# Reading the moving operand of the split products from the last column to the first, in a hybrid decoder layer on one core

## The chip, the cores and the metric

The kernel runs on one core of one Trainium2 chip. Its metric is the device time of one launch in microseconds; three timed runs of the kernel before have a median of 2824.08 us (2821.2 to 2825.72). The core's engines work side by side, each through a queue of its own: TensorE (PE, with its weight loads as PEld) does matrix products, VectorE (DVE) and ScalarE (ACT) work element by element, GpSimd (POOL) and SyncE (SP) mostly issue transfers. TensorE reads its operands from SBUF and writes its sums to banks of PSUM, 128 partitions by 512 fp32 columns each.

## The reference

One step of a decoder layer for a prompt of 2048 tokens and for eight samples of four tokens each, with a model width of 1024, in fp32. What matters here are the dense products:

```python
q, k, v, g, glr, z, xbc, dt_raw = jnp.split(hn @ lw['w_in'], cuts, axis=-1)
...
mixed = jnp.concatenate([o_gla, y], axis=-1).astype(hn.dtype) @ lw['w_out']
...
q = (hn @ w_xq).reshape(b, t, XA_HEADS, XA_HEAD_DIM).astype(jnp.float32)
s = jnp.einsum('bthd,bmhd->bhtm', q, mk.astype(jnp.float32)) * (XA_HEAD_DIM ** -0.5)
p = jax.nn.softmax(s, axis=-1)
o = jnp.einsum('bhtm,bmhd->bthd', p, mv.astype(jnp.float32)).reshape(b, t, D_MODEL)
return o.astype(hn.dtype) @ w_xo
...
f = (jax.nn.silu(hf @ lw['w_gate']) * (hf @ lw['w_up'])) @ lw['w_down']
```

Between them stand a gated linear attention and a state space scan in chunks, norms and activations. The results are the layer's output for both groups and the states that are carried on.

## The kernel before, in words

**Split products.** An fp32 operand x is kept as two parts of the type fp32r, a larger one (ScalarE's copy, `xh`, `whi`, `r` or `s`) and a smaller one (VectorE's difference between x and the larger, `xl`, `wlo`, `e` or again `s`, `r`). A product is then the sum of three matmuls, larger by larger, larger by smaller, smaller by larger. The helper `three` (L132) issues them: L134, L135 and L136, each with the stationary operand (`wh` or `wl`, 128 x 128) loaded first and the moving operand (`ah` or `al`) streamed past it, 256 to 512 columns, into the same columns of one PSUM bank. Only the first of a sum overwrites the bank; the others add to it.

**First part of the program (to about 854 us).** The prompt goes through in blocks of 512 tokens. For each, `fm` and `tm` (L542, L683) make the input projection into four banks `acc`: `fm` streams the tokens past the weights, `tm` the weights past the tokens. In between stand the pieces of the memory tokens' keys and values (`memory`, L349, banks `mx`, 256 columns), folds of the attention weights (`folds`, L438 and `last_folds`, L471), and the scans in plain fp32.

**Second part.** The output projection, the attention's scores and values, and the three products of the feed-forward part are done in passes over one kind of work each. A unit of it is a product of 2 x 2 blocks made of seven block products in place of eight, with sums and differences of blocks as operands; the results of the seven gather in the banks `accA` (two buffers), `accB` and `accC`. The moving operands, weights in `r` and `e`, have 512, 384 or 272 columns. One loop over `order` issues the matmuls of a block product through `three`, then calls the steps that empty the banks (`evs`), split the next operands (`part`) and bring in side work such as the transposes at L1858 and the samples. The order of issue on each engine follows this program text, pinned by `pin`.

**Waits.** The framework derives the waits from which tiles an instruction reads and writes. A matmul can wait on a semaphore itself; one with more waits than it can hold has an EVENT_SEMAPHORE instruction ahead of it in TensorE's queue. TensorE also waits for itself in places, on its own semaphore.

Of the kernel before, what the change touches and what calls it, by code (L numbers as in the profile page):

```python
# [42 lines left out]
def hymba_kernel(ctx: ExitStack, tc: tile.TileContext, a: dict, o: dict, dbg: dict | None = None):  # L43
# [87 lines left out]

    def three(ps, wh, wl, ah, al, start, stop, more=False):  # L132

        nc.tensor.matmul(ps, lhsT=wh, rhs=ah, start=start, stop=False, skip_group_check=more)  # L134
        nc.tensor.matmul(ps, lhsT=wh, rhs=al, start=False, stop=False, skip_group_check=more)  # L135
        nc.tensor.matmul(ps, lhsT=wl, rhs=ah, start=False, stop=stop, skip_group_check=more)  # L136
# [212 lines left out]
    def memory():  # L349
      with ExitStack() as mctx:  # L350
# [47 lines left out]
        for which, weights in enumerate((a["w_xk"], a["w_xv"])):  # L398
            for u in range(8):
                _, wh, wl = wload(weights[u], 2, pm if u % 2 else None, raws=pm)  # L400
                ps = mxt()
                for kt in range(KT):
                    k0 = kt * P
                    three(ps[:, 0:MEM], wh[:, k0:k0 + P], wl[:, k0:k0 + P], mh[:, kt], ml[:, kt], kt == 0, kt == KT - 1)
                raw = mt_([P, MEM], "kraw", bufs=2)
                nc.vector.tensor_tensor(raw, ps[:, 0:MEM], rbm, op=ALU.mult)
                nc.gpsimd.dma_start(out=kv[which, u], in_=raw)
                yield
# [29 lines left out]
    def folds():  # L438
# [3 lines left out]
        def fold_qk(n, h, Kh, Kl):  # L442
            pss = [acct() for _ in range(2)]
            _, wh, wl = wload(a["w_xqT"][n, h])
            for kt in range(4):
                c = (kt % 2) * MEM
                for d in range(2):
                    k0 = d * 512 + kt * P
                    three(pss[kt // 2][:, c:c + MEM], wh[:, k0:k0 + P], wl[:, k0:k0 + P], Kh[:, d], Kl[:, d], d == 0, d == 1)
            for u in range(2):  # L450
                t = pa2.tile([P, 512], F32, name="fold", bufs=2)
                for k in range(2):
                    kt = 4 * n + 2 * u + k
                    nc.scalar.activation(t[:, k * MEM:(k + 1) * MEM], pss[u][:, k * MEM:(k + 1) * MEM], AF.Copy, scale=gq[:, kt:kt + 1])
                c = (h % 2) * MEM
                nc.gpsimd.dma_start(out=wqk[h // 2, 2 * n + u][:, :, c:c + MEM], in_=t.rearrange("p (k m) -> p k m", m=MEM))
# [14 lines left out]
    def last_folds():  # L471
# [32 lines left out]
        for i in range(8):  # L504
            h, n = divmod(i, 2)
            if i + 1 < 8:
                split(i + 1)
            wh, wl = ws[n]
            pss = [mxt() if i == 7 else acct() for _ in range(2)]
            for mt in range(2):  # L510
                for d in range(2):
                    ms = slice(mt * P, (mt + 1) * P)
                    three(pss[mt], xc[:, 0, h, d, ms], xc[:, 1, h, d, ms], wh[d], wl[d], d == 0, d == 1)
            for mt in range(2):
                names = "fold", "fold", "fraw", "fh", "fl"
                t = pa2.tile([P, 512], F32R, name=names[(2 * i + mt) % 5], bufs=2 if (2 * i + mt) % 5 < 2 else None)
                nc.scalar.copy(f(t), pss[mt])
                nc.gpsimd.dma_start(out=wvo[n, h][:, mt], in_=f(t))
            yield
# [1746 lines left out]
    for e, (n, i) in enumerate(order):  # L2266
# [46 lines left out]
        ps = banks[n, {1: "B", 3: "C", 5: "C"}.get(i, "A")]  # L2313
# [134 lines left out]
```

## Time and profile before

| | |
|---|---|
| timed runs, median | 2824.08 us (2821.2 to 2825.72, 3 runs) |
| profiled execution, span from the first to the last instruction | 2826.9 us |
| mean granted TensorE clock | 0.991 |
| TensorE busy / its weight loads | 2737.6 us / 2366.6 us |
| VectorE / ScalarE / GpSimd busy | 2080.6 us / 1472.1 us / 536.4 us |
| TensorE instructions (matmuls) | 15,207 |
| DMA | 512.17 MB, 181 GB/s on average |

The profiled execution has no time of its own beside its span, which is 0.1% over the timed median. A row of the groups by line reads: line, engine, operation, tile written <- tiles read, shape (contraction*rows, then partitions x columns of the result) and count, then busy microseconds, mean nanoseconds of one, and idle time ahead of them. Matmuls are pipelined: the duration of one runs from its start to a modelled end and overlaps the next, so what one adds to the time is the distance from its start to the next start. A row of the timeline begins with its start and its duration in microseconds. A row of the view by stretches reads: stretch, its length, busy time and count of PE, then of PEld, then granted clock, DMA share and GB/s.

### The profile page before, as it was taken

How to read it: one execution, taken by the hardware profiler on the slowest of the kernel's cores; microseconds unless marked ns; L12 is line 12 of the kernel's file. 1: busy time of each engine (PE TensorE's matmuls, PEld its weight loads, DVE VectorE, ACT ScalarE, POOL GpSimd, SP SyncE). 2: the span in 40 equal slices, each digit the busy share in tenths (PEclk: the TensorE clock that was granted, in tenths of full speed). 3: DMA queues.
4: the chain of work that ended last, by engine and by line, in shares of the span. 5: the costliest groups of instructions: out<-in, count | busy, mean ns of one | idle time of the engine just before them, and what ended most of it. 6: DMA issues, size and time to landing. Idle time of an engine off the chain costs nothing.

```text
span 2826.9 us, 41830 instructions
## 1 busy us (share of the span) xinstructions
PE 2737.6 (97%) x15207; PEld 2366.6 (84%) x15207; DVE 2080.6 (74%) x3831; ACT 1472.1 (52%) x2921; POOL 536.4 (19%) x722
## 2 busy tenths in 40 slices
PE   8999999999998999999899999999999999999998
PEld 8987887787876878878799888899999997788786
DVE  7677677776757787677888787767677878574776
ACT  5545554554546687777755434434445555353432
POOL 2142332321322321015321210001000001000011
PEclk9999999999999999999999999999999999999999
DMA  7345535343266886468765567775244436464765
GB/s 254 116 139 187 150 104 159 117 132 89 82 206 232 283 284 225 147 189 252 266 211 184 176 243 239 256 253 176 97 138 174 151 120 209 176 211 99 236 156 128
DMA packets 151102, 512.17 MB, mean 181 GB/s; under 512 B 18176, under 2 KB 29488, under 8 KB 137328
## 3 DMA queue, kind: packets, MB, share of 16 engines
q1 hardware_dynamic: 94560, 331.81, 35.7%
q0 software_dynamic: 44240, 152.82, 17.0%
q10 hardware_dynamic: 12096, 24.86, 2.7%
q8 instruction: 120, 1.97, 0.3%
q14 instruction: 86, 0.70, 0.1%
HBM read 365.76 MB, written 143.67 MB: 180 GB/s over the span
## 4 chain that ended last, share of the span: by engine, by line
PE 76%; DVE 11%; ACT 5%; issue 3%; DMA 3%; POOL 1%; DVEq 0%; SPq 0%; POOLq 0%; ACTq 0%
PE accA L134 9%; PE accA L135 9%; PE accA L136 9%; PE accC L134 5%; PE acc L134 5%; PE acc L136 5%; PE acc L135 5%; PE accC L136 5%; PE accC L135 5%; PE accB L134 2%; PE accB L136 2%; PE accB L135 2%; DVE s L1665 2%; DVE sum L1645 1%; ACT r L1734 1%
## 5 line engine op out<-in xcount | busy, mean ns | idle before, releaser
L134 PE MATMUL accA<-r,s 128*128 128x512 f32 (+2 forms) x1792 | 637.6, 356 | 20.0 <-ACT r L1734 8.6
L136 PE MATMUL accA<-r,s 128*128 128x512 f32 (+2 forms) x1792 | 629.1, 351 | 2.8 <-DVE s L1665 2.7
L135 PE MATMUL accA<-r,s 128*128 128x384 f32 (+2 forms) x1472 | 502.8, 342 | 1.7 <-DVE r L1738 1.7
L134 PEld LDWEIGHTS accA<-r,s 128*128 128x128 f32 x1792 | 338.7, 189 | 72.6 <-ACT r L1734 12.2
L1663 ACT ACTIVATE s<-sum 128x512 fp32r<-128x512 f32 (+1 forms) x456 | 282.6, 620 | 220.1 <-DVE sum L1645 107.5
L136 PEld LDWEIGHTS accA<-r,s 128*128 128x128 f32 x1792 | 339.1, 189 | 34.0 <-DVE s L1665 4.0
L134 PE MATMUL accC<-r,s 128*128 128x512 f32 (+2 forms) x896 | 319.7, 357 | 8.8 <-ACT sg L1972 3.1
L1665 DVE TENSOR_TENSOR s<-sum,s 128x512 fp32r<-128x512 f32 (+1 forms) x456 | 305.7, 677 | 20.2 <-ACT s L1663 19.9
L136 PE MATMUL accC<-r,s 128*128 128x512 f32 (+2 forms) x896 | 314.8, 351 | 0.0
L135 PEld LDWEIGHTS accA<-r,s 128*128 128x128 f32 x1472 | 278.8, 189 | 19.0 <-DVE r L1738 2.9
L1665 DVE TENSOR_TENSOR s<-raw,s 128x512 fp32r<-128x512 f32 (+1 forms) x342 | 234.0, 684 | 51.5 <-ACT s L1663 50.4
L135 PE MATMUL accC<-r,s 128*128 128x384 f32 (+2 forms) x736 | 251.9, 342 | 0.5 <-DVE r L1738 0.5
L1663 ACT ACTIVATE s<-raw 128x512 fp32r<-128x512 f32 (+1 forms) x342 | 213.3, 624 | 72.7 <-PE accC L136 50.7
L128 ACT ACTIVATE whi<-wraw 128x1024 fp32r<-128x1024 f32 (+2 forms) x140 | 128.8, 934 | 187.3 <-PE acc L135 111.8
L134 PEld LDWEIGHTS accC<-r,s 128*128 128x128 f32 x896 | 170.1, 190 | 37.2 <-ACT s L1663 6.9
L129 DVE TENSOR_TENSOR wlo<-wraw,whi 128x1024 fp32r<-128x1024 f32 (+2 forms) x140 | 153.5, 1108 | 50.9 <-ACT whi L128 50.2
L136 PEld LDWEIGHTS accC<-r,s 128*128 128x128 f32 x896 | 170.0, 190 | 15.5 <-DVE s L1665 0.4
L142 POOL TENSOR_TENSOR rs<-ms,nhalf 128x1 f32<-128x1 f32 (+4 forms) x125 | 111.9, 896 | 361.2 <-DVE ms L140 344.9
L134 PE MATMUL acc<-xh,whi 128*128 128x512 f32 (+1 forms) x464 | 168.9, 365 | 8.7 <-ACT xh L289 8.4
L136 PE MATMUL acc<-xh,wlo 128*128 128x512 f32 (+1 forms) x464 | 164.9, 357 | 1.7 <-DVE wlo L129 1.7
L135 PE MATMUL acc<-xl,whi 128*128 128x512 f32 (+1 forms) x464 | 164.5, 356 | 0.2 <-DVE xl L290 0.2
L1645 DVE TENSOR_TENSOR sum<-raw 128x512 f32<-128x512 f32 (+1 forms) x228 | 156.5, 686 | 3.6
(698 smaller groups left out, 5876.5 us busy)
## 6 DMA issues: line engine op xcount, KB each, us to landing
raw<-in_w_gu_dram SPq DMA_DIRECT2D x66, 1024.0 KB, 4.9
wraw<-in_w_in_fm_dram SPq DMA_DIRECT2D x52, 512.0 KB, 3.7
wraw<-in_w_in_tm_dram SPq DMA_DIRECT2D x48, 512.0 KB, 3.9
st<-in_w_down_dram SPq DMA_DIRECT2D x37, 512.0 KB, 6.0
aT<-og POOLq DMA_DIRECT2D x22, 768.0 KB, 4.8
raw<-aT SPq DMA_DIRECT2D x16, 1024.0 KB, 6.2
out_y_dram<-y POOLq DMA_DIRECT2D x28, 512.0 KB, 6.2
yp<-y POOLq DMA_DIRECT2D x28, 512.0 KB, 6.3
```

What stands on the lines that cost most here:

```text
L128: last[0] = nc.scalar.activation(hi[:, cs], raw[:, cs], AF.Copy)
L129: nc.vector.tensor_tensor(lo[:, cs], raw[:, cs], f(hi)[:, cs], op=ALU.subtract)
L134: nc.tensor.matmul(ps, lhsT=wh, rhs=ah, start=start, stop=False, skip_group_check=more)
L135: nc.tensor.matmul(ps, lhsT=wh, rhs=al, start=False, stop=False, skip_group_check=more)
L136: nc.tensor.matmul(ps, lhsT=wl, rhs=ah, start=False, stop=stop, skip_group_check=more)
L142: nc.gpsimd.tensor_tensor(out=rs[:rows, :cols], in0=ms[:rows, :cols], in1=nhalf[:rows, :cols], op=ALU.pow)
L1645: nc.vector.tensor_tensor(t[out], x, y, op=o)
L1663: nc.scalar.activation(h3, v, AF.Copy)
L1665: return lambda: nc.vector.tensor_tensor(l3, v, f(h3), op=ALU.subtract)
L1734: nc.scalar.activation(hi, v, AF.Copy)
```

## The change

In `three`, ahead of the three matmuls, the accumulator and the two moving operands are replaced by views of themselves whose columns run backwards: the access starts at the last column and goes on with step -1. The stationary operands stay. Since the moving operand and the result are reversed alike, each column's sum lands where it did before.

```diff
@@ -131,6 +131,7 @@
 
     def three(ps, wh, wl, ah, al, start, stop, more=False):
 
+        ps, ah, al = (t[:, ::-1] for t in (ps, ah, al))
         nc.tensor.matmul(ps, lhsT=wh, rhs=ah, start=start, stop=False, skip_group_check=more)
         nc.tensor.matmul(ps, lhsT=wh, rhs=al, start=False, stop=False, skip_group_check=more)
         nc.tensor.matmul(ps, lhsT=wl, rhs=ah, start=False, stop=stop, skip_group_check=more)
```

Every call of `three` is reached, 12,672 matmuls. Other matmuls are left as they are. The added line moves L134 to L136 to L135 to L137 in the changed file.

The order of instructions on each engine is the same before and after. What differs is where TensorE waits for its own earlier work. One such place is the passes of the second part, where a block product ends in `accA` and the next begins in `accB`. Before:

```order
L134 MATMUL accA<-r_8425,s 128x512
L135 MATMUL accA<-e_8426,s 128x512
L136 MATMUL accA<-r_8425,s 128x512
L134 MATMUL accB<-r_8151,s 128x512
L135 MATMUL accB<-r_8151,s 128x512
L136 MATMUL accB<-r_8151,s 128x512
```

With the change:

```order
L135 MATMUL accA<-r_8425,s 128x512
L136 MATMUL accA<-e_8426,s 128x512
L137 MATMUL accA<-r_8425,s 128x512
L135 MATMUL accB<-r_8151,s 128x512 [waits PE_49]
L136 MATMUL accB<-r_8151,s 128x512
L137 MATMUL accB<-r_8151,s 128x512
```

The matmuls stand as they did; the first one into `accB` now waits on TensorE's own semaphore. Over the program 114 matmuls gain such a wait and 71 groups lose theirs, most of the latter at the transposes of L1858; the waits of the other engines are the same.

## The prediction

> **What bounds the kernel now.** I read the page from the top: the busy shares, then the chain that ended last, then the groups by line and shape, then stretches of the timeline in which matmuls follow each other without a break. The first two say which engine sets the time.
>
> ```profile
> span 2826.9 us, 41830 instructions
> PE 2737.6 (97%) x15207; PEld 2366.6 (84%) x15207; DVE 2080.6 (74%) x3831; ACT 1472.1 (52%) x2921; POOL 536.4 (19%) x722
> PE 76%; DVE 11%; ACT 5%; issue 3%; DMA 3%; POOL 1%; DVEq 0%; SPq 0%; POOLq 0%; ACTq 0%
> PE accA L134 9%; PE accA L135 9%; PE accA L136 9%; PE accC L134 5%; PE acc L134 5%; PE acc L136 5%; PE acc L135 5%; PE accC L136 5%; PE accC L135 5%; PE accB L134 2%; PE accB L136 2%; PE accB L135 2%; DVE s L1665 2%; DVE sum L1645 1%; ACT r L1734 1%
> ```
>
> TensorE is busy for 97% of the span; only 2826.9 - 2737.6 = 89 us are left in which it does nothing. The chain lies on it for 76%, and nearly all of that share is L134, L135 and L136: the three matmuls of the function that the change touches. Nothing else comes near: VectorE is at 74%. So what those matmuls take more or less goes to the end nearly whole.
>
> Next, how many they are, from one view for each line, grouped over the whole span:
>
> ```profile
> 0.00:2827.00 2827.00, 1509.67 (x4224) 800.51 (x4224) 0.99 0.56 181
> 0.00:2827.00 2827.00, 1490.60 (x4224) 800.57 (x4224) 0.99 0.56 181
> 0.00:2827.00 2827.00, 1490.27 (x4224) 799.70 (x4224) 0.99 0.56 181
> ```
>
> These are L134, L135 and L136 in that order: 4224 each, 12,672 of the 15,207 matmuls. Counted by width in the program's order, 5976 have 512 columns, 3696 have 384, 2424 have 272 and 576 have 256, together 5,285,760 columns of the moving operand. Their durations overlap, so a duration is no price. The price of a matmul in a full stream is the distance from one start to the next, and the timeline shows it at three widths:
>
> ```profile
> 99.57 0.28 PE L134 MATMUL mx<-mh,whi 128*128 128x256 f32 x1
> ...
> 102.30 0.28 PE L136 MATMUL mx<-mh,wlo 128*128 128x256 f32 x1
> ...
> 1899.56 0.33 PE L134 MATMUL accA<-r,s 128*128 128x384 f32 x1
> ...
> 1905.11 0.33 PE L136 MATMUL accA<-r,s 128*128 128x384 f32 x1
> ...
> 2601.09 0.39 PE L134 MATMUL accB<-r,s 128*128 128x512 f32 x1
> ...
> 2605.66 0.39 PE L136 MATMUL accC<-r,s 128*128 128x512 f32 x1
> ```
>
> Between the two rows of each pair lie 23, 32 and 20 steps: 2.73 / 23 = 0.1187 us, 5.55 / 32 = 0.1734 us, 4.57 / 20 = 0.2285 us. From the first and the last, one column costs (228.5 - 118.7) / 256 = 0.429 ns, and a matmul has a fixed part of 118.7 - 256 x 0.429 = 8.9 ns; the middle one should then take 384 x 0.429 + 8.9 = 173.6 ns, and takes 173.4. So the split products come to 5,285,760 x 0.429 ns = 2268 us of columns and 12,672 x 8.9 ns = 113 us of fixed parts, 2381 us or 84% of the span. Columns per nanosecond are the bound, and the change alters how each column is fetched and stored.
>
> **The change, part by part.** Nothing is added and nothing moves. The program keeps its instructions, the order on every engine is the same, the widths, the buffers, the weight loads and the DMAs too. What alters is the step of three access patterns in each of the 12,672 matmuls, from +1 to -1, with the start at the last column: two reads of a moving operand in SBUF, and the write of the result into PSUM. Three terms:
>
> First, *the read of the moving operand*. Every matmul of this kernel reads with step +1 (one pair of tiny ones has two runs of 32), so no row shows what step -1 costs. The widths 256, 272, 384 and 512 all divide by 16, so the reversed stream meets the same elements in the same neighbourhoods, in the opposite sense. Lower end: 0, the row of each width stays as it is. Upper end: the nearest rows of a matmul whose columns go through more slowly are those that are not split into fp32r parts, beside one of equal width that is:
>
> ```profile
> L135 PE MATMUL mx<-ml,whi 128*128 128x256 f32 x128 | 36.1, 282 | 0.0
> L824 PE MATMUL mx<-xw,Bt 128*128 128x256 f32 x64 | 17.8, 395 | 0.0
> ```
>
> The plain fp32 record takes 395 - 282 = 113 ns more at 256 columns, 0.441 ns for each, so it streams at half the pace. If a reversed column cost that much more, it would be 5,285,760 x 0.441 = 2331 us. I can exclude a gain here: a column is needed whichever way it is read. I take 0: the three widths lie on one straight line to 0.2 ns, so the stream runs at a steady pace per column, with no sign of a step where a matmul begins at another place.
>
> Second, *the write of the result*. The same ends, 0 and 2331 us, and they do not add, since read and write run side by side in the stream. I take 0 too, with less trust: each element goes to an address next to the one before, as it does now.
>
> [...]
>
> Third, *waits*. The built program differs in one more thing: TensorE waits for itself at other places. In 114 matmuls, each the first into its bank, a wait for an earlier matmul is added, and 71 others drop theirs (38 groups at L1858 among them). The matmul waited for lies 19 to 153 places back; even 19 of the narrowest are 19 x 0.1187 = 2.3 us, while a matmul of 512 columns takes 0.39 us, so it has ended. A wait that a matmul can't hold itself is an instruction of its own in the queue:
>
> ```profile
> L134 PEldq EVENT_SEMAPHORE  x119: 51/51/51, 30.4 to 2813.7; - x119
> L1858 PEldq EVENT_SEMAPHORE  x66: 51/51/51, 904.1 to 1431.0; - x66
> ```
>
> At 51 ns the bounds are 114 x 51 ns = +5.8 us if each of the added ones stood bare, and -1.7 us for the 34 instructions of this kind that the built program has fewer. What hides them is the stream itself: the matmul ahead of such an instruction occupies the array for at least 0.1187 us, and a wait that has already ended takes 51 ns of the queue beside it. I take 0. If that cover were gone, the first matmul of such a bank would be late, by 51 ns each, and the sum stays within these few microseconds.
>
> Sum: 2826.9 + 0 + 0 + 0 = 2826.9 us of span. That execution has no other time than its span; the median of the three timed runs, 2824.08, lies 2.8 us under it, and I keep this distance: 2824 us.
>
> **The rivals.**
>
> *Half pace.* [...] It decides from the first reversed matmul, and takes the place of everything else, for VectorE with its 2080.6 us then only waits. Price: 2268 us at 0.429 ns for each column, or 2331 us by the fp32 row, less up to the 89 us of idle time, since operands that are late now would be ready. 2824 + 2268 - 89 = 5003 to 2824 + 2331 = 5155; I name 5070. [...] Against it: the addresses are neighbours all the same.
>
> *A price for each turn.* The stream keeps its pace, but each matmul pays once for starting at the high end. The bound is the fixed part that it has now: doubled, 12,672 x 8.9 ns = +113 us, 2937 us. For it: the fixed part is the only thing in these rows that belongs to a start. Against: 8.9 ns are some 21 columns, little room for anything that could be missed.
>
> *It does nothing.* Both sides are reversed, so the lowered program may stream forward again. Then 2824 us, for another reason than mine. The built program does hold step -1, which speaks against it.
>
> *Faster.* The granted clock is the only thing that could give time back:
>
> ```profile
> core 0: 2826.9 us, clock 0.991
> ```
>
> (1 - 0.991) x 2826.9 = 25 us are lost to a lower clock. If the changed waits closed some of the gaps behind which it falls, perhaps a third of that comes back: 2816 us. Nothing in the change aims there.
>
> **How the numbers follow.** What a measurement of this kernel can tell from no change is 0.2%, 5.6 us. My forecast, a stream that keeps its pace, has 0.53; that it does nothing, 0.05; half pace 0.26; a price for each turn 0.10; faster 0.06. So faster 0.06, same 0.53 + 0.05 = 0.58, slower 0.26 + 0.10 = 0.36. The likeliest case has a range of its own, 2817 to 2832 (the wait bounds of -1.7 and +5.8 us and the spread of the timed runs, 2821.2 to 2825.72). Forecast, no effect, turns and faster together hold 0.74, which leaves out too much, so the range has to reach the half pace: 2815 to 5155. It is wide because the cost is a switch: I expect hardly any time between 2950 and 4950.
>
> **What would show it.** In the profile of the changed kernel: the start distances of 384 and 512 columns at 0.173 and 0.2285 us, and mean durations of 393 to 399 ns for the 128x512 rows into accA, mean my forecast; 0.34 and 0.45 us mean half pace, with TensorE at nearly 100% of a span that is 80% longer. A distance that grows by the same few nanoseconds at all widths is the turn. Weight loads stay at 186 to 190 ns in each case, since they are not reversed. I am wrong if the distance between starts grows in proportion to the width. I am wrong in a lesser way if the distances stay and the idle time before the first matmul of a bank grows: then the added waits are not free.

## The result, and the profile after

| | before | with the change |
|---|---|---|
| timed runs, median | 2824.19 us (2821.2 to 2825.72, 4 runs) | 2851.66 us (2848.23 to 2853.62, 4 runs) |
| profiled execution, span | 2826.9 us | 2850.1 us |
| TensorE busy / its idle time | 2737.6 us / 89.3 us | 2768.6 us / 81.5 us |

The ratio is 1.0100, with a 95% interval of 1.0088 to 1.0112: the change costs 27.5 us, far outside what the forecast of no change allowed and far below the half-pace rival. The page of the changed kernel, in the rows that the prediction showed of the kernel before:

```profile
span 2850.1 us, 41796 instructions
PE 2768.6 (97%) x15207; PEld 2377.7 (83%) x15207; DVE 2077.6 (73%) x3831; ACT 1472.3 (52%) x2921; POOL 535.1 (19%) x722
PE 80%; DVE 10%; DMA 3%; ACT 3%; issue 2%; POOL 1%; DVEq 0%; POOLq 0%; SPq 0%; ACTq 0%
L135 PEld LDWEIGHTS accA<-r,s 128*128 128x128 f32 x1792 | 340.0, 190 | 73.8 <-ACT r L1735 10.3
```

Its span and granted clock, from the view by cores:

```profile
core 0: 2850.1 us, clock 0.992
```

The loss is TensorE's alone. It is busy for 31.0 us more with the same 15,207 matmuls; VectorE, ScalarE and GpSimd are within 3.0 us of where they were, the granted clock is 0.992 beside 0.991, and a weight load takes 190 ns beside 189 in the same row before. TensorE's idle time falls by 7.8 us, so this much of the 31.0 us only fills gaps and 23.2 us reach the span. These are figures of one execution each: runs below whose distances are those of the kernel before have a TensorE busy for 2729.6 (e10) to 2734.1 us (e4). In the chain of waits TensorE's share grows from 76% to 80%: some work that used to be waited for now ends before the matmuls do.

The prediction named the distance from one matmul's start to the next as the row that decides. The timeline of the changed kernel, as pairs of a first and a last row of an unbroken stretch (start, duration, engine, line, operation):

```profile
100.35 0.28 PE L135 MATMUL mx<-mh,whi 128*128 128x256 f32 x1
...
103.05 0.28 PE L137 MATMUL mx<-mh,wlo 128*128 128x256 f32 x1
...
1959.77 0.34 PE L136 MATMUL accA<-r,s 128*128 128x384 f32 x1
...
1962.97 0.34 PE L136 MATMUL accA<-r,s 128*128 128x384 f32 x1
...
2601.09 0.40 PE L137 MATMUL accA<-r,s 128*128 128x512 f32 x1
...
2605.76 0.40 PE L136 MATMUL accC<-r,s 128*128 128x512 f32 x1
```

They lie 23, 18 and 20 steps apart: 2.70 / 23 = 117.4 ns, 3.20 / 18 = 177.8 ns, 4.67 / 20 = 233.5 ns. Before it was 118.7, 173.4 and 228.5 ns. So 256 columns cost what they did, 384 columns 4.4 ns more and 512 columns 5 ns more.

Since a few stretches could mislead, I took the same distance over the whole trace: from each split matmul to the next one of the same width, at full granted clock, without the distances that hold a gap (over 160 ns at 256 and 272 columns, 200 at 384, 260 at 512). The means, in ns, with the number of distances in the trace before; the runs below are compared by them:

| columns | before | with the change | distances |
|---|---|---|---|
| 256 | 118.4 | 118.5 | 540 |
| 272 | 125.7 | 125.5 | 2303 |
| 384 | 173.7 | 177.8 | 3498 |
| 512 | 229.5 | 233.4 | 5589 |
| of these to 880 us / 880 to 2450 us / later | 231.6 / 227.5 / 229.4 | 233.4 / 233.4 / 233.4 | |

Two things stand out. The price is a few nanoseconds for a matmul of 384 or 512 columns and, on average, nothing for 256 and 272 (at 272 columns it isn't nothing at every place: in the first 880 us the distance that begins with the second of the three products grows from 123.7 to 127.8 ns, and the one that begins with the third falls from 125.7 to 124.3). And the changed kernel has one distance at 512 columns wherever it is in the program, while the kernel before had three: 227.5 ns in the steady part, more elsewhere. So the price at 512 columns is 5.9 ns in the steady part, from 880 to 2450 us, where all the products of 384 columns lie and pay 4.1 ns, and less outside it. By the counts of the prediction, 5976 x 3.9 ns + 3696 x 4.1 ns = 38 us of distances; TensorE's busy time has 31 us of it, and the time 27.5 us.

### The profile page after: what moved, and what is told of

It reads as the page before. It is cut to its first block, busy times and chain, and to the rows that moved or that the text cites. A ratio compares the mean times of both kernels' runs of the same rounds, so it can differ in the third digit from the quotient of the medians.

```text
span 2850.1 us, 41796 instructions
## 1 busy us (share of the span) xinstructions
PE 2768.6 (97%) x15207; PEld 2377.7 (83%) x15207; DVE 2077.6 (73%) x3831; ACT 1472.3 (52%) x2921; POOL 535.1 (19%) x722
## 4 chain that ended last, share of the span: by engine, by line
PE 80%; DVE 10%; DMA 3%; ACT 3%; issue 2%; POOL 1%; DVEq 0%; POOLq 0%; SPq 0%; ACTq 0%
PE accA L135 10%; PE accA L136 10%; PE accA L137 10%; PE acc L135 6%; PE acc L136 6%; PE acc L137 6%; PE accC L135 5%; PE accC L136 5%; PE accC L137 5%; PE accB L135 3%; PE accB L137 3%; PE accB L136 3%; DVE s L1666 2%; DVE sum L1646 1%; PE mx L1859 1%
## 5 line engine op out<-in xcount | busy, mean ns | idle before, releaser
L135 PE MATMUL accA<-r,s 128*128 128x512 f32 (+2 forms) x1792 | 646.9, 361 | 18.5 <-ACT r L1735 6.8
L137 PE MATMUL accA<-r,s 128*128 128x512 f32 (+2 forms) x1792 | 637.9, 356 | 1.8 <-DVE s L1666 1.8
L136 PE MATMUL accA<-r,s 128*128 128x384 f32 (+2 forms) x1472 | 511.0, 347 | 2.0 <-DVE r L1739 2.0
L135 PEld LDWEIGHTS accA<-r,s 128*128 128x128 f32 x1792 | 340.0, 190 | 73.8 <-ACT r L1735 10.3
L137 PEld LDWEIGHTS accA<-r,s 128*128 128x128 f32 x1792 | 340.0, 190 | 36.3 <-DVE s L1666 2.9
L135 PE MATMUL accC<-r,s 128*128 128x512 f32 (+2 forms) x896 | 322.5, 360 | 8.4 <-ACT sg L1973 3.6
L137 PE MATMUL accC<-r,s 128*128 128x512 f32 (+2 forms) x896 | 317.8, 355 | 0.0
L136 PEld LDWEIGHTS accA<-r,s 128*128 128x128 f32 x1472 | 279.6, 190 | 20.4 <-DVE r L1739 2.9
L1666 DVE TENSOR_TENSOR s<-raw,s 128x512 fp32r<-128x512 f32 (+1 forms) x342 | 233.4, 682 | 53.7 <-ACT s L1664 52.8
L136 PE MATMUL accC<-r,s 128*128 128x384 f32 (+2 forms) x736 | 254.6, 346 | 0.3 <-DVE r L1739 0.3
L135 PEld LDWEIGHTS accC<-r,s 128*128 128x128 f32 x896 | 169.0, 189 | 38.5 <-ACT sg L1973 7.4
L137 PEld LDWEIGHTS accC<-r,s 128*128 128x128 f32 x896 | 169.2, 189 | 16.7
L135 PE MATMUL acc<-xh,whi 128*128 128x512 f32 (+1 forms) x464 | 169.7, 367 | 9.3 <-ACT xh L290 9.2
L137 PE MATMUL acc<-xh,wlo 128*128 128x512 f32 (+1 forms) x464 | 165.7, 359 | 1.6 <-DVE wlo L129 1.6
L136 PE MATMUL acc<-xl,whi 128*128 128x512 f32 (+1 forms) x464 | 166.6, 360 | 0.2 <-DVE xl L291 0.2
L135 PE MATMUL accB<-r,s 128*128 128x512 f32 (+2 forms) x448 | 159.1, 355 | 0.0
```

The costliest lines, as they stand in the source:

```text
L1666: return lambda: nc.vector.tensor_tensor(l3, v, f(h3), op=ALU.subtract)
```

## The experiments

All are variants of the kernel before, with one edit each; e14 and e17 have the change beside theirs. Distances are the means described above.

### Which of the three terms: read, write, or waits

e1 reverses the moving operands alone, e2 the result alone.

```diff
+        ah, al = (t[:, ::-1] for t in (ah, al))     (e1)
+        ps = ps[:, ::-1]                            (e2)
```

> Only the moving operands are read backwards; the result is written forwards, so its columns stand in reversed order in the banks and the output's values are not the layer's; the work is the same, and TensorE's waits are those of the kernel before. Theory A (the read of the moving operand costs a few ns for each matmul of 384 and 512 columns): the whole loss is here, 2851 us, start distances near 233 ns at 512 columns and 176 to 182 ns at 384. Theory B (the backward write into PSUM costs it): as before, 2824 us, 227 and 173 ns. Theory C (the moved waits of TensorE on itself): as before, 2824 us.

> Only the result is written backwards; the operands are read forwards, so again the output's values are not the layer's. TensorE's waits are exactly those of the changed kernel. Theory A (read): 2824 us, distances 227 and 173 ns. Theory B (write): 2851 us, 233 and 176 to 182 ns. Theory C (waits): 2851 us with the distances of a stream unchanged at 227 and 173 ns and more idle time ahead of the first matmul of a bank.

e1 took 2851.91 us, ratio 1.0101 (1.0086 to 1.0116); e2 took 2821.92 us, ratio 0.9994 (0.9985 to 1.0004). The timelines, e1 first:

```profile
999.67 0.40 PE L137 MATMUL accA<-r,s 128*128 128x512 f32 x1
...
1002.94 0.40 PE L136 MATMUL accC<-r,s 128*128 128x512 f32 x1
...
1959.78 0.34 PE L137 MATMUL accC<-r,s 128*128 128x384 f32 x1
...
1962.98 0.34 PE L137 MATMUL accA<-r,s 128*128 128x384 f32 x1
```

3.27 / 14 = 233.6 ns and 3.20 / 18 = 177.8 ns: the changed kernel's distances. Then e2, first its busy times from the page, then a pair of its timeline:

```profile
PE 2732.2 (97%) x15207; PEld 2362.9 (84%) x15207; DVE 2076.2 (74%) x3831; ACT 1472.4 (52%) x2921; POOL 535.9 (19%) x722
```

```profile
1959.72 0.33 PE L136 MATMUL accA<-r,s 128*128 128x384 f32 x1
...
1962.84 0.33 PE L136 MATMUL accA<-r,s 128*128 128x384 f32 x1
```

3.12 / 18 = 173.3 ns: the distance of the kernel before, and a TensorE busy for 2732.2 us. The whole loss is the read of the moving operand. The write of the result from last to first costs nothing, and since the program of e2 has the changed kernel's waits and that of e1 those of the kernel before, the moved waits cost nothing either. The runs from e3 on that take columns in another order do so in the read and the result alike; that their loss is the read's too is carried over from e1 and e2 and not shown for each.

### What in the read: steps inside four columns, steps between them, groups of 16

Four fp32 columns are 16 bytes. e3 reverses the order of these groups and keeps the columns inside forward; e4 does the opposite; e5 is e3 with groups of 16 columns (64 bytes).

```diff
+        ps, ah, al = (t.rearrange("p (a b) -> p a b", b=4)[:, ::-1] for t in (ps, ah, al))       (e3)
+        ps, ah, al = (t.rearrange("p (a b) -> p a b", b=4)[:, :, ::-1] for t in (ps, ah, al))    (e4)
+        ps, ah, al = (t.rearrange("p (a b) -> p a b", b=16)[:, ::-1] for t in (ps, ah, al))      (e5)
```

> Read and write alike go through the columns in groups of four (16 bytes): the groups from last to first, the four within a group forwards. If the price hangs on the direction in which the stream goes through memory as a whole, it stays: 2851 us, 233 ns at 512 columns. If it hangs on the order within a group or on step -1 as such, it goes: 2824 us, 227 ns. If a pattern of two levels has a price of its own, the time is above 2855 us, with distances above 240 ns.

> The converse of the run with groups from last to first: the groups of four columns go forwards, the four within each backwards. If the direction of the stream as a whole sets the price: 2824 us, 227 ns at 512 columns. If the order within a group or step -1 does: 2851 us, 233 ns. If a pattern of two levels has a price of its own: above 2855 us, as in that run.

> Groups of 16 columns (64 bytes) from last to first, forwards within a group, read and write alike. Theory D (what costs is the direction in which the read as a whole goes): still 2851 us, 233 ns between starts at 512 columns. Theory J (each step back between groups of four costs its own small slot, 6.4 ns / 128 steps at 512 columns): a quarter of the steps, a quarter of the loss, 2831 us and 228.6 ns. If 64 bytes is the unit in which memory is read: 2824 us and 227 ns.

e3: 2852.77 us, 1.0101 (1.0085 to 1.0118). e4: 2823.53 us, 1.0002 (0.9993 to 1.0011). e5: 2852.13 us, 1.0102 (1.0088 to 1.0116). Distances of 384 and 512 columns: e3 177.8 and 233.4 ns, e4 173.6 and 229.5 ns, e5 176.7 and 233.8 ns. A pair of e5's timeline:

```profile
999.64 0.40 PE L136 MATMUL accA<-r,s 128*128 128x512 f32 x1
...
1002.91 0.40 PE L135 MATMUL accB<-r,s 128*128 128x512 f32 x1
```

3.27 / 14 = 233.6 ns. Going backwards inside 16 bytes is free. The cost comes with the order of the groups, and it isn't a price for each step downwards: a matmul of 512 columns has 511 of them in the changed kernel, 127 in e3 and 31 in e5, at one price.

### Whether it is the place of the start, or an address

e6 reads the second half of the columns before the first, so that the stream starts in the middle and steps back once.

```diff
+        ps, ah, al = (t.rearrange("p (a b) -> p a b", a=2)[:, ::-1] for t in (ps, ah, al))
```

> The two halves of the columns change places, each is read and written forwards: one step back in each matmul, and the start is in the middle. Theory D (direction): 2824 us, 227 ns at 512 columns. Theory S (a matmul pays for where its read starts or ends against the next one's): 2835 to 2851 us. Theory J: 2824 us.

2822.32 us, 0.9998 (0.9989 to 1.0007), 173.7 and 229.5 ns. A start elsewhere is free, and so is one step back.

The next two leave every read forward and move tiles instead. e7 shifts the moving operands of the second part by 256 bytes against the stationary ones. e8 lays the token pieces of blocks 1 to 3 out so that successive operands lie a multiple of 512 bytes apart, and moves five of the tiles `e` by 32 bytes to the same end.

```diff
+    rp0.tile([P, 64], F32, name="pad")                           (e7)
...
+        xa = pa1.tile([P, 16 * (BT + NS)], F32R, name="xa")      (e8)
...
-            h = pa1.tile([P, T], F32R, name=f"xh{kt}")
-            l = pa1.tile([P, T], F32R, name=f"xl{kt}")
+            h = xa[:, 2 * kt * T:(2 * kt + 1) * T]
+            l = xa[:, (2 * kt + 1) * T:(2 * kt + 2) * T]
...
+            for k in range(2, 7):
+                rd.tile([P, 1024], F32R, name=f"e{k}")
+            rd.tile([P, 8], F32, name="pad")
```

> The kernel before, forwards, with 64 unused columns (256 bytes) ahead of the moving operands of the second part: r0 to r6 and the first e tiles move by 256 bytes against the stationary operands s, nothing else changes. Theory W (the read of the moving operand collides in SBUF with the read of the next matmul's weights, and the addresses of the two modulo 512 bytes decide how often): distances in the second part rise from 227 to 231 ns or more at 512 columns and from 173 to 176 ns or more at 384, time 2835 to 2850 us, with nothing reversed. Rival (the direction costs by itself, addresses don't matter): 2824 us, 227 and 173 ns.

> The kernel before, forwards, with the split tokens of the first part laid out in one tile so that in blocks 1 to 3 every piece starts at the same address modulo 512 bytes as the weight tiles, and with the e tiles of the last passes moved by 32 bytes for the same reason. Theory W: the 512-column distances of the first part fall from about 231.6 to 227.5 ns, those of the last passes from 229.8 to 227.5 ns, some 2100 x 4.1 + 1700 x 2.3 ns = 12 us, 2812 us, less what is lost because a block's tokens, now one tile, can't be written before the block ahead has been read. Rival (addresses don't matter): distances unchanged, 2824 us or slower.

e7: 2822.76 us, 1.0004 (0.9995 to 1.0013), distances as before at all widths. A place 256 bytes further on against the stationary operand doesn't matter to a forward read; other distances weren't tried. e8: 2823.98 us, 1.0002 (0.9992 to 1.0011), but its distances of 512 columns fall from 231.6 to 228.8 ns in the first 880 us and from 229.4 to 226.8 ns after 2450 us. So the levels of the kernel before come from where the operands lie. It is not the moving ones alone: e8 moves the tokens, and where these are the stationary operand (1042 of the 1963 distances of the first 880 us), successive moving operands lie a multiple of 512 bytes apart before as in e8. There the kernel before has 228.7 ns where successive stationary operands lie a multiple of 512 bytes apart too, and 232.7 ns where they are off by 128 bytes, by the addresses of the built programs; in e8 it is 228.1 and 232.2 ns, with far fewer of the latter (169 in place of 700). The program is no faster for it, where W had wanted 2812 us, and TensorE, busy for 2730.3 us, isn't less busy than in e7 (2730.0 us): in the first 880 us the distances next to matmuls of another kind or width come to 240 us in e8 and 227 us in e7.

### From the end of one operand to the start of the next, or the direction itself

By now two theories were left. By T a read downwards costs by itself, at some scale above 64 bytes. By E what counts is the step from the last place read to the first place of the next operand, by its remainder to 512 bytes: it goes on by one column in a forward read and in e6, in e4 by one group of four columns (to its last column), and goes back in the changed kernel, e3 and e5. Two group sizes that keep this step tell something, one operand in three something else; e12 gives the share of each width.

```diff
+        ps, ah, al = ((t.rearrange("p (a b) -> p a b", b=64)[:, ::-1] if t.shape[-1] in (384, 512) else t) for t in (ps, ah, al))   (e9; e10: b=128)
...
-        nc.tensor.matmul(ps, lhsT=wh, rhs=al, start=False, stop=False, skip_group_check=more)                       (e11)
+        nc.tensor.matmul(ps[:, ::-1], lhsT=wh, rhs=al[:, ::-1], start=False, stop=False, skip_group_check=more)
...
+        ps, ah, al = (t[:, ::-1] if t.shape[-1] == 512 else t for t in (ps, ah, al))                                (e12)
```

> Widths 384 and 512 only: groups of 64 columns (256 bytes) are read and written from the last to the first, forward inside a group; the narrower products stay as before. The result is the same. Two theories are open. T (direction): a moving operand whose places are read downwards costs more, whatever comes before or after it; groups of 64 bytes cost as much as single columns, two halves nothing, so the scale is between 64 and 1024 bytes, and T expects a result between those: 2835 to 2852 us, distances of 512 columns at 229 to 233 ns and of 384 columns at 175 to 178 ns. E (from the end of one to the start of the next): what counts is the step from the last place read of one operand to the first place of the next, by its remainder to 512 bytes; in the kernel before it goes on by one column, read from last to first it doesn't, and neither does it with groups of 64 bytes. Here the last group ends 256 bytes into the operand and the next starts 1792 (384 columns: 1280) bytes into the next one, so that the step goes on by one column again: E expects nothing, 2819 to 2827 us, 227 and 173 ns.

> As the groups of 64 columns, with groups of 128 columns (512 bytes): three steps downwards in an operand of 512 columns, two in one of 384. E expects nothing again (2819 to 2827 us, 227 and 173 ns), since the last group ends 512 bytes into the operand and the next operand starts at a multiple of 512. T expects less than with groups of 64 columns, or as much: 2830 to 2852 us if the scale lies above 512 bytes, 2824 us if below; together with the groups of 64 columns it gives the scale.

> Of the three products only the second (wh with al) reads its moving operand from last to first and writes its result so; the first and third stay forward. The result is the same. T: only the second product costs more, by 6 ns at 512 columns and 4.5 ns at 384, as a third of the changed kernel's loss: 2830 to 2836 us, and only the distance that starts at the second product's matmul grows. E: the step from the first product's end to the second's start, and from the second's end to the third's start, no longer goes on by one column but stays at the same place by the remainder to 512 bytes; either two distances of three grow (2838 to 2845 us), or, if staying is as good as going on, none (2819 to 2827 us). A growth of the second product's alone speaks for T.

> The change for products of 512 columns alone; 256, 272 and 384 columns stay forward. From the distances of the two traces (512 columns: mean about 4.5 ns more over some 2,100 distances between 890 and 2,430 us, 4 ns over some 1,600 after it, 1 to 2 ns over some 2,000 before; 384 columns: 4.3 ns over some 3,500) the 512-column products would bring about 18 of 33 us, of which 27.4 us reached the end. Both theories: 2835 to 2843 us, 384 columns at 173 ns. If the time stays at 2824 us the loss is all the 384 columns', if it is above 2848 us all the 512 columns'.

e9: 2822.91 us, 1.0002 (0.9992 to 1.0012), and e10: 2822.24 us, 1.0000 (0.9991 to 1.0010), both with 173.7 ns at 384 columns and 229.5 and 229.4 ns at 512. e9's busy times on the page, and a pair of its timeline:

```profile
PE 2733.9 (97%) x15207; PEld 2365.4 (84%) x15207; DVE 2076.5 (74%) x3831; ACT 1472.1 (52%) x2921; POOL 536.0 (19%) x722
```

```profile
1959.79 0.33 PE L136 MATMUL accA<-r,s 128*128 128x384 f32 x1
...
1962.91 0.33 PE L136 MATMUL accA<-r,s 128*128 128x384 f32 x1
```

3.12 / 18 = 173.3 ns. Seven groups back, of 256 bytes each, are free where 31 of 64 bytes cost in full. E expected just that. T had wanted 2835 to 2852 us for e9 and missed; it is left only with a scale between 64 and 256 bytes.

e11: 2828.34 us, 1.0022 (1.0013 to 1.0032), 5.6 us over its comparison. At 512 columns, between 880 and 2450 us, the distance that begins with the second product grows from 227.4 to 232.4 ns; the first product's stays at 227.3 and the third's at 227.8. That is T's forecast; E wanted two of three, or none. Outside this stretch it is less clean: in the first 880 us the second product's grows from 231.9 to 233.9 ns, while the first's falls by 1.4 and the third's by 2.0. At 384 columns it isn't T's forecast: the second product's stays (173.8 and 173.4 ns), the third's grows by 3.1 ns and the first's by 0.9. The time is a little under T's 2830 to 2836 us.

e12: 2840.72 us, 1.0064 (1.0046 to 1.0083), distances 233.4 ns at 512 and 173.6 at 384 columns. So the 512 columns bring 18.0 of the 27.5 us, and some 9.5 us are left for the 384 columns, by difference; they had no run alone.

The next three part E and T. e13 puts the low part of five of the seven 384-column tiles 64 bytes further on, all reads forward; e14 is the same layout with all reads reversed, which makes one step between operands go on upwards; e15 takes groups of 32 columns.

```diff
-        return (rp0 if k < 2 else rp).tile([P, 2 * RW], F32R, name=f"r{PLACE[k]}")                                   (e13, e14)
+        return (rp0 if k < 2 else rp).tile([P, 2 * RW + 16 * (k > 1)], F32R, name=f"r{PLACE[k]}")
...
-                    self.at[i] = r[:, 0:RW], r[:, RW:2 * RW]
+                    self.at[i] = r[:, 0:RW], r[:, RW + 16 * (k > 1):2 * RW + 16 * (k > 1)]
...
-        rp.tile([P, 2 * RW], F32R, name=f"r{k}")
+        rp.tile([P, 2 * RW + 16], F32R, name=f"r{k}")
...
+        ps, ah, al = (t[:, ::-1] for t in (ps, ah, al))                                                              (e14)
...
+        ps, ah, al = ((t.rearrange("p (a b) -> p a b", b=32)[:, ::-1] if t.shape[-1] in (384, 512) else t) for t in (ps, ah, al))   (e15)
```

> All products read forward, as in the kernel before. In five of the seven operand tiles of the 384-column products (r2 to r6; r0 and r1 stay as they are, so that they serve as the comparison) the low part lies 64 bytes further on, so that the step from the first product's operand to the second's is off by 64 bytes by the remainder to 512, and the one from the second's to the third's by as much the other way. Behind the low part the tiles r3 to r6, and five tiles e, move by 64 to 320 bytes as well. E (what counts is the step from the last place of one operand to the first of the next): the distances of 384 columns in r2 to r6 that begin with the first and with the second product grow by some 3 to 8 ns, as those of 512 columns with such remainders are longer in the kernel before; r0 and r1 stay at 173 to 174 ns. T (only the direction counts): 173 to 174 ns in all seven. The time: E 2830 to 2845 us, T 2822 to 2832 us (the 512-column products, some of which are off too, may add to both).

> The same layout, with all operands read and results written from last to first. E: the step from the first product's operand (last read: its first column) to the second's (first read: its last column) is now 60 bytes forward by the remainder to 512, which goes on upwards as the forward read does: in r2 to r6 the distance that begins with the first product falls back to 173 to 174 ns, in r0 and r1 it stays at 177 to 178. T: nothing falls back, 176 to 182 ns in all seven, and the distances of 512 columns are 233 ns whatever the remainder; time 2849 to 2856 us.

> Widths 384 and 512 only, groups of 32 columns (128 bytes) from last to first. E: the step between two operands is off by 256 bytes by the remainder to 512, and forward reads with that remainder take 231.4 ns in the trace of before: 512 columns at 230 to 233 ns, 384 at 175 to 178, 2838 to 2852 us. T: reading downwards in steps of 64 bytes costs, in steps of 256 bytes not; either the limit lies above 128 bytes and the distances are 233 and 178 ns (2852 us), or below it and they are 227 and 173 ns (2823 us). A result without loss excludes E.

e13: 2828.62 us, 1.0021 (1.0010 to 1.0032). Its 384-column distances in the shifted tiles that begin with the first and the second product are 174.2 and 173.8 ns; the whole width has 174.4 ns. E wanted 3 to 8 ns more and gets under 1 ns. The loss of 4.5 us goes mostly with the 512 columns, 230.9 ns instead of 229.5, whose tiles moved too.

e14: 2850.11 us (two runs), 1.0094 (1.0073 to 1.0114). At 512 columns the mean is 233.4 ns, and 232 to 235 ns for each of the remainders that this layout makes, so there E falls as an explanation of the loss. At 384 columns, where the step now goes on upwards, the distance is 176.9 ns and not 173 to 174: it was 177.0 in the changed kernel, so that putting the step right brought nothing back at that place. Over the three products the shifted tiles have 175.9 ns and the unshifted two 177.6; what fell is the distance that begins with the second product, from 179.1 in the changed kernel to 174.8 ns in the shifted tiles, while the unshifted ones have 180.8. T, which wanted 176 to 182 ns in all, has no place for that. Since in e11 the price at 384 columns appeared one matmul late, a part of E can't be excluded at this width.

e15: 2841.71 us, 1.0068 (1.0051 to 1.0084). Pairs of its timeline:

```profile
1001.09 0.39 PE L135 MATMUL accA<-r,s 128*128 128x512 f32 x1
...
1002.96 0.39 PE L137 MATMUL accA<-r,s 128*128 128x512 f32 x1
...
1959.80 0.34 PE L136 MATMUL accA<-r,s 128*128 128x384 f32 x1
...
1962.96 0.34 PE L136 MATMUL accC<-r,s 128*128 128x384 f32 x1
```

1.87 / 8 = 233.8 ns and 3.16 / 18 = 175.6 ns; over the trace 232.2 and 175.9. Groups of 128 bytes cost 17.6 us over their comparison's median of 2824.15 us (19 by the ratio), some two thirds of the changed kernel's loss. E had forecast just that, the time and both distances; T had named the whole loss or none, and missed. So the scale at which reading downwards begins to cost isn't a sharp limit, and here the price also follows the address: the 288 distances of 512 columns whose next operand starts at a remainder of 384 bytes have 227.3 ns and those at 256 bytes 229.4, less than in the kernel before (231.5 and 231.4), while those at 0 have 232 to 233.

### Whether the weight load beside it matters

While a matmul streams, the weights of the next one are loaded (in the kernel before the loads are busy for 2366.6 us and the matmuls for 2737.6 us of one span of 2826.9). e16 and e17 shorten one load in three, forward and reversed. In e7 and e8 W stood for a collision with that load that hangs on addresses; here it stands for one that hangs on the time of the load.

```diff
-        nc.tensor.matmul(ps, lhsT=wh, rhs=al, start=False, stop=False, skip_group_check=more)
+        nc.tensor.matmul(ps[:64], lhsT=wh[:, :64], rhs=al, start=False, stop=False, skip_group_check=more)           (e16, e17)
...
+        ps, ah, al = (t[:, ::-1] for t in (ps, ah, al))                                                              (e17)
```

> All reads forward; the second product multiplies by only 64 of the 128 columns of its stationary operand (wh with al) and adds to the first 64 rows of the result, so that a part of the sums is left out. Its weight load, which runs beside the first product's stream, should shrink from some 190 ns to about half. It is the comparison for the next run. Distances of 512 columns 227 to 233 ns and of 384 columns 173 to 174 ns, as in the kernel before, and 2815 to 2826 us by either theory.

> The same computation with the moving operands read and the results written from last to first. W (the moving operand's read downwards costs because the stationary operand of the next product, which the build reads back to front, is read beside it; the cost lies in the time that the load takes): the distance that begins with the first product, beside which the half load runs, loses less: at 512 columns 229 to 231 ns instead of 233, at 384 columns nearer 173 than 177; those that begin with the second and the third product stay at 233 and 177 to 179. T (the read costs by itself): the three are as in the changed kernel, 233 to 234 ns at 512 columns whichever product begins, and 177 to 179 at 384. The time against the run before: W +16 to +22 us, T +25 to +29 us.

The groups by line of e17 show the shortened load, and its timeline the distance:

```profile
L136 PEld LDWEIGHTS accA<-r,s 128*64 128x64 f32 x1472 | 200.4, 136 | 21.0 <-DVE r L1739 3.4 <-DVE s L1666 0.4
```

```profile
999.61 0.40 PE L136 MATMUL accB<-e,s 128*64 128x512 f32 x1
...
1002.87 0.40 PE L135 MATMUL accC<-r,s 128*128 128x512 f32 x1
```

The load takes 136 ns in place of 190, less of a cut than the half that I had expected, and a matmul of 512 columns still 3.26 / 14 = 232.9 ns. After 2450 us, where few gaps disturb the mean, the distance that begins with the first product (beside which the short load runs) is 234.4 ns, the others 233.5 and 233.1 (distances to 323 ns taken in). Over the trace e17 has 177.8 and 233.5 ns, as the changed kernel. At 512 columns that is T's forecast. At 384 columns the mean is the changed kernel's but not its parts: the distance that begins with the first product is 175.8 ns (177.0 in the changed kernel), the second's 181.3 (179.1) and the third's 176.1 (177.2), which is neither W's near 173 nor T's 177 to 179. e17 took 2852.81 us (two runs, 6.9 us apart), 1.0110 (1.0069 to 1.0150).

e16 itself missed what both theories expected: 2830.74 us, 1.0028 (1.0017 to 1.0039), with distances of 175.2 and 230.5 ns. The forward stream became slower by 7.8 us; whether by the shorter load or by the result of 64 rows in place of 128, which goes with it, wasn't parted. Against this, its own comparison, e17 loses 22.1 us, the upper end of what W had named and less than T's 25 to 29; two runs so far apart don't decide between them. The distances speak for T at 512 columns: the reversed stream is where it was in the changed kernel, and the difference is smaller because the forward one had become slower.

## Why the prediction was wrong

**What bounds the kernel** was right, and is why 4 ns matter at all: TensorE's 97%, the 12,672 split matmuls, and the start distance as their price. That the change goes to the end nearly whole is less exact: of 31.0 us more of busy time 23.2 us reached the span of the profiled executions, and the medians of the timed runs differ by 27.5 us.

**The read of the moving operand** is the step that failed. It had no row, the bounds were 0 and 2331 us, and I took 0 because the three widths lie on a straight line, "with no sign of a step where a matmul begins at another place". That argument was about starts, and e6 (0.9998) shows that starts are indeed free. It said nothing on the direction, for every row it used had the same one. The term measures 27.5 us, that is 1% of its upper bound. That bound was taken from durations, which the prediction itself calls no price: the starts of the plain fp32 matmuls at L824 lie 216 ns apart, some 97 ns more than those of a split matmul of 256 columns, 0.38 ns for each column and some 2010 us in place of 2331. And the straight line was in part luck: the 228.5 ns mix distances of 226 to 227 ns with some of 230 to 236 ns; with the 227.5 ns of the steady part the line from 256 columns passes 384 at 173.0 ns, 0.7 ns under the 173.7 measured.

Reversing the columns changes two orders at once, and the term was taken as one. The order inside groups of four columns, 16 bytes, is free (e4, 1.0002). The order of the groups isn't: e3 reverses only that, and its ratio is 1.0101.

**The write of the result**, taken at 0 "with less trust", is 0: e2, 0.9994, with 173.3 ns at 384 columns as in the kernel before. Results written in pieces out of order cost nothing either (e6, 0.9998; e9, 1.0002).

**The waits** are 0 as forecast, by e2 (0.9994), which has them all. **Weight loads** stay at 190 ns as said.

**The rivals.** *A price for each turn* is nearest: a few nanoseconds for each matmul that the stream pays whatever its length. It had 0.10 and 2937 us from doubling the 8.9 ns. The measured price is on average 0 at 256 and 272 columns and 4 to 6 ns at 384 and 512, so it isn't the same at all widths, as that rival wanted, and a start elsewhere than at the first column costs nothing (e6, 0.9998). *Half pace*, with 0.26, was too heavy: no row gave a sign of it, and no run shows a column that takes twice as long for being read or written downwards. A matmul of 512 columns takes 233.4 ns with the change, where half pace meant 0.45 us. *Does nothing* and *faster* are out. And "the distance grows in proportion to the width" is no description either: in the steady part 512 columns pay 5.9 ns and 384 columns 4.1, but 272 columns nothing, where some 3 ns would be in proportion.

**The range** held the time, but only since it reached to 5155 us. (The lower end of the likeliest case, 2817, doesn't come out of its terms either: 2821.2 - 1.7 is 2819.5.) Around 2850 us, between the likeliest case and the turn at 2937, no case of mine had its centre; a small price for the read, between the two ends that I had written down, would have been the natural one.

**What is shown and what stays open.** Shown: the loss is the read of the moving operand; its scale lies between 64 and 256 bytes (by the ratios, single columns lose 28 us, groups of 16 and 64 bytes 29, of 128 bytes 19, and groups of 256 and 512 bytes and halves nothing within their intervals); it is carried by 384 and 512 columns; at 512 columns neither the step to the next moving operand (e11, e14) nor the length of the weight load beside it (e17, with one load in three 28% shorter) explains it. Not shown is that the direction costs by itself: this is what is left of the two theories, but it missed in e15 and at the second products of e14, where the price fell with the addresses. At 384 columns no theory fits the three products (e11, e14, e17). Open: why reading downwards at that scale costs, why 256 and 272 columns are spared on average, and whether the stationary operands, whose places count in the forward stream, have a share in it. Reading the stationary operand the other way round, which could say more on the two reads side by side, wasn't tried.

## What to carry to other kernels

Where an operand has to be taken in reversed order, reverse the side that is free: here the result in PSUM could be written from last to first at no cost (e2, 0.9994), and the moving operand read in pieces of 256 bytes or more, from the last piece to the first (e9, 1.0002; e10, 1.0000), while its columns or 64-byte pieces read downwards cost 4 to 6 ns for each matmul of 384 or 512 columns in the steady part. When a stream is 97% of the time, a term without a row deserves a case of its own at one or two per cent of the stream, since equal rows in one direction say nothing on the other. Undoing one half of an edit at a time (e1 and e2) settled within two runs what no argument from the trace could.

## What the runs showed beside this

The forward stream has levels of its own. At 512 columns it takes 226.8 ns where successive operands, moving and stationary, lie a multiple of 512 bytes apart (e8, after 2450 us), and 231.6 ns in the first part of the kernel before, where most don't in the one or the other. A reversed stream has 233.4 ns in all three stretches of the program. Before and change, in the steady part:

```profile
1000.01 0.39 PE L134 MATMUL accC<-r,s 128*128 128x512 f32 x1
...
1002.51 0.39 PE L136 MATMUL accC<-r,s 128*128 128x512 f32 x1
```

2.50 / 11 = 227.3 ns in the kernel before, and with the change, in the same part:

```profile
999.80 0.40 PE L136 MATMUL accA<-e,s 128*128 128x512 f32 x1
...
1002.84 0.40 PE L137 MATMUL accB<-r,s 128*128 128x512 f32 x1
```

3.04 / 13 = 233.8 ns. That part is where the change costs most, 6 ns for each matmul of 512 columns; in the first 880 us it costs 1.8 ns, since the stream there was already slow. Nor had I expected that a second product with half the weight columns, and so a shorter load and a result of half the rows, slows the stream (e16, 2830.74 us with PEld busy for 2206.2 us in place of 2366.6).
